# Moving the wait for the last store from the drain to the semaphore clear, in a row-sum kernel

## Chip, cores, metric

One Trainium2 chip, one core. The metric is the device time of one execution in microseconds; lower is better. Before the change: 161.77 us, median of three runs (161.68 to 161.86).

## The reference

```python
x: (32, 512, 1024) float32
np.sum(x, axis=-1).astype(np.float32)      # 16384 sums of 1024 values each
```

67.1 MB are read and 64 KB written. In the profile of the kernel before, the packets of the loads take 97.7% of the 16 DMA engines' span, VectorE is busy for 75% of it and ScalarE for 11%: a stream of loads with the arithmetic at its side.

## The kernel before

SyncE issues all loads and the last store. VectorE sums most rows, ScalarE the rest of the last ones. The input comes in pieces that get smaller towards the end, so that little work is left when the last byte has landed: the last load, 232 KB, lands at 157.838 us, and the last row sum ends 455 ns later, at 158.293. The store that ScalarE issues for the rows before, at 156.62, lands at 158.720, behind the loads. The end of the body:

```python
        # ... the last row comes in two pieces, each summed as halves
        nc.sync.dma_start(out=part, in_=rows_from(j, 1)[:, 0, :c])
        nc.sync.dma_start(out=whole[:, 1 : width + 1], in_=rows_from(j, 1)[:, 0, c:])
        hold(store(nc.scalar, 0, last), two, "its packets come behind those of the loads")
        halves(whole[:, :1], part)
        halves(sums[:, j : j + 1], whole)
        store(nc.sync, last, last + 1)          # the last store, 8 KB
```

Behind the body the framework appends a closing block. Its steps, as the trace of the kernel before has them (us from the start of the span):

- SyncE waits for the semaphores of the kernel, the store's excepted, 158.720 to 158.990. A semaphore is a counter that an engine or a transfer raises and another engine waits for: the last store raises its own sixteen times from 159.575 to 159.744, and the instruction that waits for it starts 24 ns after the last of them.
- The five engines meet in a barrier: POOL, which is GpSimd, gathers the other four at 159.070 and releases them at 159.149.
- POOL runs a drain (the profile's DRAIN, 70 ns here) and clears the kernel's ten semaphores (93 ns).
- The engines meet once more: POOL gathers at 160.067 and releases at 160.145.

A hook of the kernel edits this block: it takes the wait for the last store out of SyncE's list and gives it to POOL, so that the first barrier passes while the store is in flight, here 0.6 us ahead of the landing at 159.744:

```python
def wait_for_the_store_at_the_clear(nc):
    # ... cut: `insts` is the closing block; `wait` is taken from SyncE's list of waits
    pool = [k for k, i in enumerate(insts) if i.engine == mybir.EngineType.Pool]
    clear = next(k for k in pool if isinstance(insts[k], mybir.InstISA))
    drain = pool[pool.index(clear) - 1]
    # ...
    insts[drain] = copy.replace(
        insts[drain], sync_info=mybir.SyncInfo(on_wait=[wait], on_update=[])
    )
```

## Time and profile before

| | before |
|---|---|
| time, three runs | 161.77 us (161.68 to 161.86) |
| span of the profiled execution | 160.25 us (its time: 162.03 us) |
| last store issued / landed | 158.321 / 159.744 us |
| from the landing to the end of the span | 506 ns |

The landing is the moment at which the sixteenth increment of the store's semaphore arrives. Times with three decimals are from the trace's own records, in us from the start of the span; the views round to 0.1 or 0.01 us. The last line of the table is what the change works on. In the window from 159.7 to 160.1 us, this is what POOL does in the kernel before (columns: line, engine, operation and count: shortest/median/longest ns, first and last start in us):

```profile
L241 POOLq DRAIN  x2: 34/52/70, 159.8 to 160.0; - x2
L241 POOLq EVENT_SEMAPHORE_RANGE_CLEAR  x1: 93/93/93, 159.9 to 159.9; - x1
L241 POOLq EVENT_SEMAPHORE  x1: 17/17/17, 160.1 to 160.1; - x1
```

Two drains, one of 70 ns and one of 34, with the clear between them, all after the landing at 159.744.

### The profile page before, as it was taken

The page shows a single profiled execution, that of the slowest core. Times are in us where ns is not written, and L with a number is a line of the kernel's source. Part 1 is how long each engine was busy: PE and PEld are TensorE (multiplying, and loading weights), DVE is VectorE, ACT ScalarE, POOL GpSimd, SP SyncE. Part 2 cuts the span into 40 slices and gives each one's busy share as a digit, 9 for nine tenths or more (in the row PEclk, how much of TensorE's full clock was granted, in tenths as well). Part 3 has the DMA queues.
Part 4 walks back from the last instruction along what each step waited for, and adds up shares of the span by engine and source line. Part 5 has one row for each costly group of instructions (what it writes and reads, how often), then busy time and mean ns, then how long its engine had stood idle before and what let it go on. Part 6 is the DMA issues. An engine that isn't in the chain of part 4 may idle for free.

```text
span 160.2 us, 125 instructions
## 1 busy us (share of the span) xinstructions
DVE 120.1 (75%) x22; ACT 17.3 (11%) x31; POOL 0.2 (0%) x4
## 2 busy tenths in 40 slices
DVE  0280059960799959999499994999949998597943
ACT  3000000000000000000000000000000000596952
POOL 0000000000000000000000000000000000000000
DMA  7999996996996996996996997998969969999994
GB/s 262 458 466 515 393 523 262 523 523 262 523 523 262 523 523 262 523 523 262 523 491 294 523 458 327 523 409 376 523 262 523 523 262 523 393 393 425 409 379 112
DMA packets 2928, 67.18 MB, mean 419 GB/s; under 512 B 1264, under 2 KB 1392, under 8 KB 1520
## 3 DMA queue, kind: packets, MB, share of 16 engines
q1 hardware_dynamic: 2016, 67.12, 97.7%
q10 hardware_dynamic: 912, 0.06, 0.4%
HBM read 67.11 MB, written 0.07 MB: 419 GB/s over the span
## 4 chain that ended last, share of the span: by engine, by line
DMA 73%; DVE 25%; SPq 1%; issue 0%; DVEq 0%
DMA t<-in_x_dram 73%; DVE sums L130 24%; SPq L169 1%; SPq L210 0%; DVE t L144 0%; DVEq L241 0%
## 5 line engine op out<-in xcount | busy, mean ns | idle before, releaser
L130 DVE TENSOR_REDUCE sums<-t 128x16 f32<-128x16384 f32 (+3 forms) x9 | 116.6, 12953 | 35.5 <-DMA t<-in_x_dram 35.5
L157 ACT ACTIVATE unread<-t 128x1024 f32<-128x1024 f32 x15 | 15.2, 1010 | 139.6 <-DMA t<-in_x_dram 139.6
L144 DVE CUSTOM_DVE_ANT_0 t<-t 128x512 f32<-128x512 f32 (+2 forms) x6 | 3.5, 603 | 2.7 <-DMA t<-in_x_dram 2.6
L157 ACT ACTIVATION_READ_ACCUMULATOR unread<-t 128x1 f32 x15 | 2.8, 186 | 0.0
L157 ACT ACT_TABLE_LOAD x1 | 1.3, 1283 | 0.8 <-PEq L230 0.8
L144 DVE DVE_READ_ACCUMULATOR2_ANT sums<- 128x1 f32 x5 | 0.4, 84 | 0.0
L230 POOL MEMSET const-bfloat16-1.0<- 128x1 bf16 x1 | 0.1, 102 | 0.0
L230 POOL MEMSET const-uint8-127<- 128x1 uint8 x1 | 0.1, 102 | 0.0
L230 POOL MEMSET const-float32-0.0<- 128x1 f32 x1 | 0.1, 99 | 0.2 <-issue 0.2
L230 POOL MEMSET const-float32-1.0<- 128x1 f32 x1 | 0.1, 99 | 0.0
L144 DVE DVE_READ_ACCUMULATOR2_ANT t<- 128x1 f32 x1 | 0.1, 82 | 0.0
L208 DVE MEMSET t<- 128x1 f32 x1 | 0.1, 59 | 0.0
## 6 DMA issues: line engine op xcount, KB each, us to landing
t<-in_x_dram SPq DMA_DIRECT2D x1, 6144.0 KB, 20.9
t<-in_x_dram SPq DMA_DIRECT2D x1, 4096.0 KB, 31.3
t<-in_x_dram SPq DMA_DIRECT2D x1, 2560.0 KB, 37.3
t<-in_x_dram SPq DMA_DIRECT2D x1, 2048.0 KB, 7.1
t<-in_x_dram SPq DMA_DIRECT2D x1, 1024.0 KB, 39.3
t<-in_x_dram SPq DMA_DIRECT2D x1, 280.0 KB, 39.5
t<-in_x_dram SPq DMA_DIRECT2D x1, 232.0 KB, 39.6
t<-in_x_dram SPq DMA_DIRECT2D x6, 40.8
```

What stands on the lines that cost most here:

```text
L130: return nc.vector.tensor_reduce(out=dst, in_=src, axis=mybir.AxisListType.X, op=mybir.AluOpType.add)
L144: return nc.vector.tensor_tensor_reduce(out=src[:, :n], in0=src[:, :n], in1=src[:, n:], scale=1.0, scalar=0.0, op0=mybir.AluOpType.add, op ...
L157: nc.scalar.activation(out=unread[:, :n], in_=src, func=mybir.ActivationFunctionType.Copy, accum_out=dst,)
L169: load = nc.sync.dma_start(out=block, in_=rows_from(j, n))
L208: nc.vector.memset(whole[:, width + 1 :], 0.0)
L230: nc = _bacc.Bacc("TRN2", target_bir_lowering=False, num_devices=1)
```

## The change

The intent: the drain was thought to have nothing to do with the store, so let it run while the store flies, and let only the clear wait. The clear keeps the wait because it resets the semaphore that the store increments: in the trace of before the sixteenth increment comes at 159.744 and the reset at 159.914. The diff:

```diff
-    pool = [k for k, i in enumerate(insts) if i.engine == mybir.EngineType.Pool]
-    clear = next(k for k in pool if isinstance(insts[k], mybir.InstISA))
-    drain = pool[pool.index(clear) - 1]
-    assert isinstance(insts[drain], mybir.InstDrain)
-    info = insts[drain].sync_info
+    clear = next(
+        k
+        for k, i in enumerate(insts)
+        if i.engine == mybir.EngineType.Pool and isinstance(i, mybir.InstISA)
+    )
+    info = insts[clear].sync_info
     assert info is None or not (info.on_wait or info.on_update)
-    insts[drain] = copy.replace(
-        insts[drain], sync_info=mybir.SyncInfo(on_wait=[wait], on_update=[])
+    insts[clear] = copy.replace(
+        insts[clear], sync_info=mybir.SyncInfo(on_wait=[wait], on_update=[])
     )
```

## The prediction

> **What bounds the kernel now.** I read the page first (shares, chain), then the end of the chain in order of time, then the instructions of the closing line, because the diff touches only the closing block. The page says that the bound is the stream of loads:
>
> ```profile
> span 160.2 us, 125 instructions
> DVE 120.1 (75%) x22; ACT 17.3 (11%) x31; POOL 0.2 (0%) x4
> DMA 73%; DVE 25%; SPq 1%; issue 0%; DVEq 0%
> q1 hardware_dynamic: 2016, 67.12, 97.7%
> ```
>
> The loads' queue keeps the 16 DMA engines busy for 97.7% of the span; the chain charges the vector engine with 25% only because its reductions free the buffers that the next load waits for. POOL, the engine that the diff edits, does 0.2 us of counted work, all of it in the first half microsecond. So whatever the edit is worth is decided in the last microsecond or two, after the last byte of input has arrived. That end, from the chain in order of time and the timeline, is:
>
> ```profile
> 118.20 39.64 DMA t<-in_x_dram
> 157.84 0.05 issue
> 157.88 0.40 DVE t L144
> 158.29 0.01 DVEq L241
> ...
> 158.32 0.35 SPq L180 DMA_DIRECT2D out_dram<-sums  x1
> ```
>
> The last load lands at 157.84, the last row sum is done at 158.29, and SyncE issues the last store at 158.32. The list of DMA issues gives 1.4 us from issue to landing for that 8 KB store. The views' chain stops at the vector engine and doesn't follow the store to the end of the span, so I read the rest in the instructions of the closing line (columns: engine, operation, count: shortest/median/longest ns, first and last start in us):
>
> ```profile
> L241 SPq EVENT_SEMAPHORE  x6: 17/28/28, 158.7 to 160.2; - x6
> L241 POOLq EVENT_SEMAPHORE  x4: 17/17/17, 159.1 to 160.1; - x4
> L241 POOLq DRAIN  x3: 34/41/70, 0.7 to 160.0; - x3
> L241 SPq DRAIN  x3: 7/7/7, 159.0 to 159.3; - x3
> L241 POOLq EVENT_SEMAPHORE_RANGE_CLEAR  x1: 93/93/93, 159.9 to 159.9; - x1
> ```
>
> Rounded to 0.1 us this is too coarse for the question, so I took the same instructions from the trace's records in ns (from the span's start). SyncE checks the other semaphores at 158.72 to 159.04 while the store flies; a first barrier over the five engines is released at about 159.15; the store's sixteenth increment lands at 159.744. Then POOL alone: drain with the wait for the store 159.768 to 159.838 (70 ns), range clear 159.867 to 159.960 (93 ns), a second drain 159.989 to 160.023 (34 ns), two semaphore instructions of 17 ns at 160.067 and 160.145, and the other engines' last release waits, the latest ending at 160.250, the end of the span. From the landing to the end is 506 ns, all of it a chain with nothing beside it. The edit is in the first two links of this chain.
>
> [...] POOL issues its release at 159.149 and the drain's record begins only at 159.768, 24 ns after the landing, so 70 ns is the execution, not the wait. ([...] a two-wait semaphore instruction of SyncE at line 180 is recorded with 39046 ns, so there a wait is inside.)
>
> [...] The trace has 7 ns on SyncE, but 34, 41 and 70 ns on POOL. [...] POOL's is dearer, and the one that had to wait is the dearest of the three.
>
> [...]
>
> **The change part by part.** The instructions are the same before and after, in the same order on every engine; I compared the built programs, and what differs is one thing: the wait for the store's semaphore (at least 32) sits on the range clear and no longer on the drain ahead of it.
>
> Removed from the path: the drain now runs as soon as POOL has released the first barrier, at about 159.2, some 0.55 us ahead of the landing at 159.744. Its execution (70 ns) and the step from its end to the clear's start (159.867 less 159.838, 29 ns) lie under the flight of the store. Gross gain 70 + 29 = 99 ns.
>
> Added to the path: the clear now begins where the drain began, 24 ns after the landing, if it wakes as fast. It may wake dearer: the drain that waited took 70 ns, and POOL's two others, which waited for no semaphore of their own, 41 and 34, mean 37.5; the difference, 32 ns, may be a cost of having waited and not of draining. If so, it goes over to the clear, which then takes about 93 + 32 = 125 ns. That leaves 99 - 32 = 67 ns. I have no record that tells the two apart, so I take the middle: (99 + 67) / 2 = 83 ns, rounded to 80 ns.
>
> Moved: nothing on SyncE, the vector or the scalar engine, no load and no buffer. The second drain, the barrier after it and its releases follow the clear at the same distances, so they end earlier by what the clear gains.
>
> Sum: the span goes from 160.25 to about 160.17 us, and the time from 161.77 to 161.77 - 0.08 = 161.69 us. That is 0.05%, and half of the 0.18 us that the three runs before lie apart (161.68 to 161.86). The profile, which counts ns, should show it; the clock outside hardly can.
>
> **The rivals.** First: the wait is what costs, and the clear pays it in full or worse. A range clear that has to wait might be handled in a slower way than a drain, or begin its work only after the wait, where it now has been prepared under the drain. For it: the 29 ns between POOL's instructions, which is the same 29 before the clear and before the second drain, leaves no sign of preparation either way, and the drain's 70 ns shows that waiting may cost. Against it: the clear writes some ten semaphores within its 93 ns and nothing in it depends on the drain. If the clear lost as much as the drain's 99 ns, the time would stay at 161.77; if it lost 200 ns, it would be 161.87. Both are inside the 2% band.
>
> Second: the store isn't the last to arrive, so that moving its wait gains nothing, and the end is set by the barrier. For it would speak a barrier release near the landing. Against it: the release is at 159.15 and the landing at 159.74, a slack of 0.59 us, far over the 99 ns in play. I give this almost nothing; the time would be 161.77.
>
> Third: the gain is real but swallowed after the span. The reported time is 161.77 for a span of 160.2, so 1.5 us lie outside; if something there ends on a clock of its own, an earlier end of the span is lost. Nothing in the views speaks for or against it. The time would again be 161.77.
>
> Fourth: the executions differ by more than the edit. The profiled run took 162.03 us, 0.26 more than the median. A load stream of 160 us that shifts by 0.2% moves the time by 0.3 us, four times the gain, in either direction.
>
> **Range and chances.** The mechanism allows 161.65 to 161.87 (a gain of 0.12 to a loss of 0.1). Scatter of the loads is the larger part: the three runs and the profiled one span 161.68 to 162.03, 0.35 us in width. I take a width of 0.55 us, a little over one and a half times that, about the guess, which gives 161.42 to 161.97. 2% would be 3.2 us, six times the whole 506 ns that follow the landing; even if POOL's part of the end took no time at all, the kernel couldn't be faster by 2%, and to be slower by 2% the clear would have to take over 30 times its 93 ns. [...]
>
> **What would show it.** In the changed kernel's closing line: three POOL drains, of which the middle one starts near 159.2 and none takes 70 ns; the range clear's start about 24 ns after the landing of the store and 30 ns or less is added to its 93; from landing to the end of the span about 506 - 80 = 426 ns. A middle drain that still starts after the landing, or a clear of over 190 ns, would make the prediction's mechanism wrong; a clear of 125 ns would say that waiting has a price of its own, one of 93 that it hasn't. The part up to the store's issue should be unchanged in kind, and any difference there is scatter.

The middle of 99 and 67 ns, 83, was rounded to 80 ns, and 161.77 less 0.08 gave 161.69 us. On the vector engine's 25%: in the trace of before SyncE's load issues wait for its reductions six times, 92.3 us in total.

## The result, and the profile after

| | before | changed |
|---|---|---|
| time, median of six runs | 161.81 us (161.68 to 162.53) | 161.78 us (161.48 to 162.14) |
| ratio, 95% interval | | 0.9994 (0.9971 to 1.0016) |
| profiled span | 160.250 us | 160.241 us |
| last store issued / landed | 158.321 / 159.744 us | 158.412 / 159.834 us |
| from the landing to the end | 506 ns | 407 ns |

A ratio is the mean time of one kernel's fast runs over that of the other's of the same rounds, so it is not quite the ratio of the medians quoted. The slowest lies 0.5% above the fastest of its kernel before and 0.4% after. The three runs of before from the start are among the six.

The two spans differ by only 9 ns, although the part that was changed became 99 ns shorter. The reason is upstream: in this execution the store was issued 91 ns later, because the last load came later. The end of the chain after, in order of time (start us, length us, what), beside that in the prediction:

```profile
118.59 39.34 DMA t<-in_x_dram
157.93 0.05 issue
157.97 0.40 DVE t L145
```

The last load lands at 157.93 where it was 157.84: nothing of this is in the diff, and it takes back nearly the whole gain in this one pair of traces. This is why the closing block has to be read from the landing and not from the start of the span.

What lies behind the span is the time of the profiled execution less its span: 162.03 less 160.250 before and 162.02 less 160.241 after, 1.78 us in both. So in these two executions nothing of the 99 ns was lost behind the span.

The changed kernel's POOL in two windows, the first from 159.2 to 159.5 us, ahead of the landing at 159.834:

```profile
L242 POOLq EVENT_SEMAPHORE  x1: 17/17/17, 159.2 to 159.2; - x1
L242 POOLq DRAIN  x1: 70/70/70, 159.3 to 159.3; - x1
```

and the second from 159.7 to 160.1 us:

```profile
L242 POOLq EVENT_SEMAPHORE_RANGE_CLEAR  x1: 93/93/93, 159.9 to 159.9; - x1
L242 POOLq DRAIN  x1: 34/34/34, 160.0 to 160.0; - x1
L242 POOLq EVENT_SEMAPHORE  x1: 17/17/17, 160.1 to 160.1; - x1
```

The drain has moved to 159.3, and it still takes 70 ns though it waits for nothing now. The clear takes 93 ns though it waits. In the records (ns after the landing):

| | before | changed |
|---|---|---|
| drain ahead of the clear | 24 to 94 | -513 to -443 |
| clear | 123 to 216 | 24 to 117 |
| second drain | 245 to 279 | 146 to 180 |
| end of the span | 506 | 407 |

The clear has taken the drain's place 24 ns after the landing, and all behind it moved by 99 ns.

### The profile page after: what moved, and what is told of

It reads as the page before. It is cut to its first block, busy times and chain, and to the rows that moved or that the text cites. A ratio compares the mean times of both kernels' runs of the same rounds, so it can differ in the third digit from the quotient of the medians.

```text
span 160.2 us, 125 instructions
## 1 busy us (share of the span) xinstructions
DVE 120.1 (75%) x22; ACT 17.3 (11%) x31; POOL 0.2 (0%) x4
## 4 chain that ended last, share of the span: by engine, by line
DMA 73%; DVE 25%; SPq 1%; issue 0%; DVEq 0%
DMA t<-in_x_dram 73%; DVE sums L131 24%; SPq L170 1%; SPq L211 0%; DVE t L145 0%; DVEq L242 0%
```

## The experiments

Theory: after the landing there is one chain on POOL; whatever doesn't need the store can lie under its flight for nothing, and what needs it costs its full length. Rivals: an instruction that waits pays for the waiting (the 32 ns of the prediction); the drain prepares POOL for the clear; an earlier end of the span doesn't reach the time. All kernels gave correct results and run at a clock of 1.0. Edits are given against the changed kernel and are shortened.

### The changed kernel without the drain

```diff
+    del insts[drain]          # POOL's drain ahead of the clear
```

> The drain ahead of the clear is taken out of the changed kernel; the clear still waits for the store. Theory (the drain lies under the store's flight, so its length doesn't matter any more): the clear starts 24 ns after the landing and takes 93 ns, and the span ends 407 ns after the landing, as in the changed kernel. Rival (the drain prepares POOL for the clear, so that the clear is only cheap behind it): the clear takes 30 ns or more longer, and the end is 440 ns or more after the landing.

Measured: the clear starts 24 ns after the landing and takes 93 ns; the end comes after 408 ns. The drain can be left out altogether and nothing moves, so in the changed kernel it is off the path. It does not prepare the clear.

### Twenty more drains, behind the wait and ahead of it

```diff
+    more = [copy.replace(plain, name=...) for n in range(20)]
+    # behind: the wait goes back to the first drain; ahead: it stays on the clear
+    insts[clear:clear] = more
```

> The wait is on the drain, as before, and 20 more drains stand between it and the clear. Theory: they all lie on the path. A drain takes 34 or 70 ns plus a step of 29 ns, so the end comes 506 + 20 x 63 = 1766 ns to 506 + 20 x 99 = 2486 ns after the landing, and the time outside is longer than before by 1.3 to 2.0 us (0.8 to 1.2%). The profile tells which of 34 and 70 ns a drain behind another drain takes. Rival (what ends the span isn't what ends the time): the span grows by as much, the time outside by less than half of it.

> The wait is on the clear, as in the change, and the same 20 drains stand ahead of it. Theory: they begin at the barrier's release, some 0.44 us ahead of the point at which the clear could start (159.858 less 159.420 in the changed kernel), so that 0.44 us of their length are hidden: the end comes about 407 + 1260 - 438 = 1229 ns after the landing if each takes 63 ns with its step (1949 ns if 99), 0.54 us less than with the same drains behind the wait. The clear no longer waits. Time outside: 0.7 to 1.5 us over before. Rival (a sequencer wait costs as much wherever it is): same end as with the drains behind the wait.

POOL with the drains behind the wait, from 159.4 to 161.4 us (landing at 159.443):

```profile
L250 POOLq DRAIN  x21: 59/59/70, 159.5 to 161.2; - x21
L250 POOLq EVENT_SEMAPHORE_RANGE_CLEAR  x1: 93/93/93, 161.3 to 161.3; - x1
```

and with the same drains ahead of it, from 159.05 us to the landing at 159.581, then from 159.6 to 161.02:

```profile
L248 POOLq DRAIN  x6: 59/59/70, 159.1 to 159.5; - x6
```

```profile
L248 POOLq DRAIN  x15: 59/59/59, 159.6 to 160.8; - x15
L248 POOLq EVENT_SEMAPHORE_RANGE_CLEAR  x1: 93/93/93, 160.9 to 160.9; - x1
```

Behind: 21 drains, all after the landing, and the end 2240 ns after it, 1734 ns more than before. Ahead: six start before the landing, 15 after it, and the end comes after 1722 ns, 518 ns sooner than with the same drains behind. The first drain starts 509 ns ahead of the landing where it else starts 24 ns after it; that is 533 ns, and 15 ns of it are lost again: from the last drain's end to the clear's start it is 45 ns where the clear has a wait that is long satisfied (160.869 to 160.914) and 30 ns where it has none (161.264 to 161.294). So a wait isn't quite free, by one pair of traces, but in the changed kernel this lies under the flight.

The expectation had left open whether a drain takes 34 or 70 ns. It is 70 for the first two of a row and 59 for the others, 86 ns with the step.

Time outside: behind, 163.74 us, ratio 1.0110 (1.0091 to 1.0129), which of the 161.94 us that before took on average in these rounds is 1.78 us for 1.73 in the profile; ahead, 163.05 us, ratio 1.0069 (1.0052 to 1.0087), 1.12 us for 1.22. What is added at the end of the span reaches the time: the rival that it is swallowed outside falls for delays; for gains see the last versions below.

### Four more drains ahead of the wait

```diff
+    more = [copy.replace(plain, name=...) for n in range(4)]
+    insts[clear:clear] = more
```

> The wait is on the clear and four more drains stand ahead of it. Theory: four times 63 to 99 ns is 252 to 396 ns, less than the 0.44 us that are free there, so nothing of it shows: the clear starts 24 ns after the landing, the end comes 407 ns after it. Rival (a drain costs wherever it stands): the end comes 250 to 400 ns later, at 660 to 800 ns.

Measured: the five drains fill 159.295 to 159.719, the landing is at 159.803, the clear starts 24 ns after it, and the end comes after 413 ns. The 6 ns over 407 are in the second drain, behind the clear, which took 40 ns here. Some 350 ns of added work cost only these 6 ns at that place.

### The store's wait back with SyncE

```diff
-    nc.at_finalize(wait_for_the_store_at_the_clear)
```

> The whole hook is left out, so the store's wait goes back to SyncE's list of waits ahead of the first barrier. Theory: the barrier, the drain and the clear all follow the landing. From SyncE's last wait to POOL's first chance at the drain the kernel before took 159.168 less 158.983, about 0.2 us, and the drain's 70 ns and a step of 29 ns come on top: the end comes 506 + about 250 = 750 ns after the landing, 0.35 us later than with the change. Time outside: 0.25 us over before (0.15%), hardly to be told. Rival (the barrier is hidden under something else): the end stays at 506 or less.

Measured: the end comes 870 ns after the landing, 120 ns later than expected; time 162.47 us, ratio 1.0031 (1.0013 to 1.0050), about 0.50 us for 0.36 in the profile. The direction is the theory's; the size I had underrated. SyncE in the window from 159.9 to 160.3 us, with the landing at 159.998:

```profile
L241 SPq EVENT_SEMAPHORE  x2: 28/28/28, 160.0 to 160.1; - x2
L241 SPq DRAIN  x2: 7/7/7, 160.1 to 160.2; - x2
```

The store's wait stands in the fourth of SyncE's five wait instructions, not at the last place as I had assumed. Behind it come another wait (160.077) and two drains (160.142, 160.200), then POOL's gather (160.232) and release (160.311) and only then its drain, at 160.392. That is 394 ns after the landing, against 24 in the kernel before: 370 more, less 6 for a drain of 64 ns. The instruction that waits for the store here has two waits and is recorded with 28 ns, from 17 ns after the landing; in the kernel before, SyncE's two-wait instruction at line 180 is recorded with 39046 ns, from 118.691 to 157.737. So the length of a record held a wait in one case and not in the other.

### The closing barrier ahead of the clear

```diff
+    insts.append(insts.pop(clear))     # the clear is the last instruction of the block
```

> From the changed kernel, POOL's part of the closing barrier is put ahead of the clear, so that the clear with its wait is the very last instruction. Theory (everything that doesn't need the store can lie under its flight): the second drain, the barrier and the releases, 290 ns from the clear's end to the span's end, are over before the landing; the end comes 24 + 93 = 117 ns after it, 0.39 us less than before, 0.24% of the time. Rival (what stands behind the program brings it back[...]): the profile shows the 117 ns, the time outside gains less than 0.15 us.

Measured: the end comes 117 ns after the landing, as expected: 24 and the clear's 93. POOL from 158.9 us to the end at 159.591, the landing at 159.474:

```profile
L245 POOLq EVENT_SEMAPHORE  x3: 17/17/17, 158.9 to 159.2; - x3
L245 POOLq DRAIN  x2: 34/49/64, 159.0 to 159.1; - x2
L245 POOLq EVENT_SEMAPHORE_RANGE_CLEAR  x1: 93/93/93, 159.5 to 159.5; - x1
```

POOL's drains and its release are over at 159.2, the other engines' release waits at 159.3; the clear stands alone behind the landing. Time: 161.64 us, ratio 0.9986 (0.9966 to 1.0006), or 0.23 us for 0.39 in the profile. The interval holds both the theory's 0.39 and zero, so by this series alone the rival isn't refuted. The profiled execution shows that a part comes back: it took 161.44 us for a span of 159.591, so 1.85 us lie outside the span, where all versions with the barrier behind the clear have 1.78 to 1.79. That is some 0.06 us of the 0.39; what takes them wasn't looked for.

### The clear in three

```diff
+    # semaphores 99..105, 107..108 and 106; only the last part has the wait
+    insts[clear : clear + 1] = parts
```

> The clear of ten semaphores is cut into three: seven and two ahead of the wait, and the store's own alone behind it. Theory (the clear's 93 ns grow with the number of semaphores: in the trace they fall in groups of three or four, some 20 ns apart): the clear of one takes about 93 - 40 = 50 ns, and the end comes about 365 ns after the landing. Rival (fixed cost): it takes 93 ns, and the end comes 407 ns after the landing. A clear of seven would be about 80 ns by the theory, 93 by the rival.

POOL's closing line, in one piece (its first drain, at 0.7 us, is far from the end):

```profile
L255 POOLq DRAIN  x3: 34/41/70, 0.7 to 160.2; - x3
L255 POOLq EVENT_SEMAPHORE_RANGE_CLEAR  x3: 44/45/73, 159.7 to 160.2; - x3
```

Measured: 73 ns for seven semaphores, 45 for two, 44 for one; the end comes 359 ns after the landing, 48 less than with the clear whole. The clear's length grows with what it clears, so the rival of a fixed cost falls. It doesn't grow by one semaphore at a time: in the records the resets come in groups of at most four, about 21 ns apart (the ten as four, four and two, where the expectation has "three or four"; the seven as four and three; one or two together), and the lengths follow the number of groups. That they go by groups is a reading of four sizes, not tested further.

### Both together

```diff
+    insts[clear : clear + 1] = parts
+    insts.append(insts.pop(clear + 2))   # the store's own clear comes last
```

> Both together: the clear in three, the barrier ahead of the last one, so that behind the landing there is only the clear of the store's own semaphore. If its length grows with the number: end 24 + 50 = 74 ns after the landing; if it is fixed: 117 ns. The time outside is 0.39 to 0.43 us below before if what the profile shows reaches it, and the two versions can't be told apart by it.

Measured: the end comes 68 ns after the landing, 438 ns sooner than before. Time: 161.38 us, ratio 0.9971 (0.9952 to 0.9990), or 0.47 us. Of the profiled execution 1.84 us lie outside the span, so here too some 0.05 us of the 0.44 come back there.

### Which drain is dear

By my reading of the program's listing, the drain ahead of the clear is not like POOL's other two in the closing line: it alone carries a mark, with the range of the semaphores that are to be reset. What the mark does isn't shown by a run; what it costs is. Two kernels have it plain, with the wait on it as before, alone or with 20 more:

```diff
+    plain = copy.replace(plain, is_reset_sema=None, reset_range_start=None, reset_range_stop=None)
     # the wait on this drain, none on the clear; then 0 or 20 copies
```

> The wait is on the drain as before, but the drain has lost the mark with which the program gives it the range of semaphores to be reset, which neither of POOL's two other closing drains carries. Theory (the 70 ns belong to this kind of drain, not to having waited, and not to its place): it takes 34 to 41 ns as the plain ones do, and the end comes 506 - 36 = about 470 ns after the landing. Rival (its place behind the barrier makes it dear): 64 to 70 ns and 500 to 506 ns.

> As the twenty drains behind the wait, with all 21 of them plain. There 21 marked drains took 70 ns (the first two) and 59 ns, at a pitch of 86 ns, and the end came 2240 ns after the landing. Theory (the kind decides): 34 to 41 ns each, a pitch of about 64 ns, and the end about 470 + 20 x 64 = 1750 ns after the landing. Rival (place or row of drains decides): 59 ns again and 2240 ns.

POOL first with one plain drain that waits, from 160 to 160.25 us (landing at 160.024), then with 21, from 159.6 to 160.9 us (landing at 159.604):

```profile
L251 POOLq DRAIN  x2: 34/34/34, 160.0 to 160.2; - x2
L251 POOLq EVENT_SEMAPHORE_RANGE_CLEAR  x1: 93/93/93, 160.1 to 160.1; - x1
```

```profile
L251 POOLq DRAIN  x21: 34/34/34, 159.6 to 160.8; - x21
```

The plain drain that waits takes 34 ns at the same place where the marked one took 70, and the end comes after 470 ns as expected. All 21 take 34 ns at a pitch of 61 ns; the end comes after 1687 ns (expected about 1750; I had put the step at 30 ns, it is 27). So it is the kind of drain that makes 70 of 34, and waiting adds nothing to its recorded length. Place moves it less: in the closing line, over all runs, a marked drain took 59 to 70 ns, a plain one 34 to 41.

### The change and the last version again, side by side

> The changed kernel itself, once more, for the time outside: theory 0.1 us below before (ratio 0.9994), far inside an interval of some 0.4% width; the profile shows the end 407 ns after the landing, the clear 93 ns.

> The version with the store's own clear as the last instruction, once more, beside the change on the same chip: theory 0.44 us below before (0.9973) and 0.34 us below the change; the end 68 ns after the landing. If the first series was luck, its ratio is not below 1 this time.

Measured: the change 161.81 us, ratio 0.9995 (0.9982 to 1.0008), its end 407 ns after the landing with a clear of 93; the other version 161.65 us, ratio 0.9978 (0.9964 to 0.9992), or 0.36 us below before, its end 68 ns after the landing. This version's POOL, first from 159.4 to 159.9 us, then behind the landing at 159.925:

```profile
L256 POOLq DRAIN  x2: 34/52/70, 159.4 to 159.7; - x2
L256 POOLq EVENT_SEMAPHORE_RANGE_CLEAR  x2: 45/59/73, 159.5 to 159.6; - x2
L256 POOLq EVENT_SEMAPHORE  x2: 17/17/17, 159.8 to 159.8; - x2
```

```profile
L256 POOLq EVENT_SEMAPHORE_RANGE_CLEAR  x1: 44/44/44, 159.9 to 159.9; - x1
```

Two series now have it below before with the whole interval. Against the change on the same chip its six runs average 161.59 to 161.81 us, 0.22 us less where the profile says 0.34 (and 1.83 us lie outside the span against 1.79). It has the lowest ratio of all that were run, about a quarter of a percent below before, though the interval of the version with the whole clear last overlaps with its own: a clear of 44 ns is all that is left behind the landing. It gives up that the other engines stand in a barrier until the clear is done (before, POOL's release came at 160.145, behind the clear's end at 159.960; here it starts at 159.8, ahead of the clear at 159.9); its twelve executions ran without a fault, but what relies on that order elsewhere was not tested.

## Why the prediction was right, point by point

- **The place of the gain** was right. The drain lies under the store's flight; leaving it out changes nothing (408 ns), and four more at its place are free (413 ns).
- **The clear starts where the drain did**: right to the nanosecond, 24 ns after the landing in both.
- **The size of the gain** was mis-sized in one term: "the difference, 32 ns, may be a cost of having waited and not of draining". It is neither. The 70 ns belong to the drain with the reset mark: it took 70 without waiting, and a plain drain took 34 with waiting. The three drains that I compared were of two kinds, which the listing of the program would have told and the profile's row, "x3: 34/41/70", does not. The clear took 93 ns and not up to 125, so the gain is the gross 70 + 29 = 99 ns and not the middle of 83. With it the sign that I named for the changed kernel, that no drain takes 70 ns, was wrong as well.
- **The sum**: 161.69 us was said and 161.78 measured, in the range. The range was made wide for the scatter of the loads, 0.55 us for a gain of 0.08, so that the time fell into it says little for the mechanism; the nanoseconds behind the landing do. The gain that the profile counts, 0.1 us, is an eighth of what the six runs of before lie apart (161.68 to 162.53), and both series' intervals contain 1. That the time itself fell is therefore not shown by these series. That the end of the span reaches the time is shown by larger doses: +1.73 us gave +1.78, +1.22 gave +1.12, and -0.44 gave -0.47 and -0.36.
- **The rivals**: that the clear pays for the wait fell by its 93 ns; that the barrier sets the end fell by the drains ahead of the wait, where 0.5 us are free; that the gain is swallowed outside fell by the doses, and for the change itself by the 1.78 us outside the span on both sides. (The "1.5 us" of the prediction set the median of three runs against the span of another, slower execution; of one and the same it is 1.78.) That executions differ by more than the edit was right: in the one pair of traces, a load that came later took back 90 of the 99 ns.

## What to carry to other kernels

Only what needs the last transfer should stand behind the wait for it: in the last version that left a clear of 44 ns, and 68 ns from the landing to the end where before had 506. In this kernel everything else, the closing barrier too, could go ahead of the wait and was nearly free as long as it fitted into the transfer's flight, here about 0.5 us behind the first barrier; the barrier gave back some 0.05 us behind the span. Read such a change from the event that releases it (the landing) and not from the span, since the stream ahead scattered more (the six runs of before lie 0.85 us apart) than the edit was worth (0.1 us). And before a duration is put down to waiting, check in the program that the instructions compared are of one kind.
